# A hybrid decoder layer in fp32 on one core: loads of the last output projection in another ring, the first up weights split ahead, one down product moved to the change of token halves

## The chip, the cores and the metric

The kernel runs on one NeuronCore of a Trainium2 chip. The core has a matmul engine (TensorE, written PE; its weight loads are PEld), a vector engine (VectorE, DVE), an engine for functions and copies (ScalarE, ACT), a general one (GpSimd, POOL) and a queue engine (SyncE, SP) that issues most of the transfers between memory (DRAM) and the on-chip buffer (SBUF). PSUM, eight banks of 128x512 fp32, takes the sums of the matmuls. The engines run beside each other; each works through its own list of instructions in order and waits on semaphores where it needs another's result.

The metric is the time of one execution on the device in microseconds (us). The profile is that of one execution; times in it count from the start of its span.

## The reference

One layer over 2048 tokens of width 1024, all in fp32:

```
h = rmsnorm(x, norm1_w);  p = h @ w_in                  # 1024 -> 3840 columns
o = concat(hgrn2(p[:, :2048]), rwkv7(p[:, 2048:]))      # two recurrent mixers, 512 columns each
x = x + o @ w_out                                       # 1024 x 1024
u = rmsnorm(x, norm2_w) @ w_up                          # 1024 -> 2 x 2816
u = causal_conv(u, conv_w, width 3) + conv_b
x = x + (silu(gate(u)) * val(u)) @ w_down               # 2816 -> 1024
return rmsnorm(x, final_norm_w)
```

The change touches `o @ w_out` for the last 512 tokens, the start of `@ w_up`, and one part of `@ w_down`.

## The kernel before

**Numbers in two parts.** A matmul operand in fp32 is split into a high part (a cast to fp32r on ACT, line 243 or 236) and a low part (the difference, on DVE, line 244 or 237). `mm3` (lines 257 to 261) makes one 128x128 by 128x512 product out of three matmuls: high x high (L259) and the two products of a high and a low part (L260, L261).

**Token blocks and halves.** The 2048 tokens are four blocks of 512 (`b` 0 to 3); blocks 0 and 1 are token half 0, blocks 2 and 3 half 1.

**Phase 1** (`phase1`) makes the mixers for all blocks and the output projections of blocks 0 to 2. Its last output projection, of block 2, runs with matmuls named `pj` beside the end of the mixers of block 3. The mixers' results go to DRAM as `oT[3]`; the last two such stores, of tiles `osq` and `yo`, are issued by POOL. All its SBUF tiles are given back at its end, and the tiles of the second part lie over the same bytes. A new tile waits until every tile of phase 1 that it overlaps has been read for the last time, the whole tile and not only the bytes shared.

**The last output projection** (lines 1142 to 1208, matmuls `wacc`) is that of block 3. For two column halves `dh` and eight k tiles in the order 0, 1, 4, 5, 2, 3, 6, 7 it loads a tile of `w_out` (ring "w") and, in the first half, a tile of `oT[3]` (ring "o"). `rings` puts them in the four slots each of `Bl[2]` and `Bh[2]`, 8 KB tiles whose bytes lie over `hh` and `hl`, the operands that the last `pj` matmuls read. `take` and `weights` split them: `oT` into `Bh[3]`, `Bl[3]`, `Bh[5]`, `Bl[5]`, the weights into `woh`, `wol` (three buffers each, pool `op`). The function `load` chains these loads in the order of the text. Three small loads of `conv_w` and `conv_b` (`crow`) stand ahead of all of them in the program; two transposes of `crow` (`cps`, line 1207) stand behind the last `wacc` matmul.

**The up projection** (`run`, lines 1296 to 1391) works on one token half at a time as a 2x2 block product with seven block products instead of eight (Strassen-Winograd). For each of 22 column tiles `fb` of each half (`n` = 0 to 43) four raw tiles of `w_up` (`uraw`, six buffers, pool `wr2`) give seven operands a11, a12, s2, s1, s3, a22, s4, each split into `uwh`, `uwl` (five buffers) and multiplied with one of the seven prepared activations `Bh[i]`, `Bl[i]`: 12 matmuls a product, 84 an iteration. The accumulators are `ua`, `ub`, `ud`. The last two products and the convolution and gate of iteration n are `late`, called after the first product of iteration n + 1. The gate is a chain on ACT and DVE (lines 1374 to 1388) that ends in stores of `gd`, the input of the down projection.

`build(h, i, kk)` loads a quarter of activation i of half h into the ring `br` (six buffers) and splits it to `Bh[i]`, `Bl[i]`. For half 0 part of this is done in the last output projection and the rest in `run`'s beginning and first iteration. For half 1 the 28 quarters are rebuilt in iterations 21 and 22: a `B[i]` may be overwritten when its last product of half 0 is done; `rebuild(2)` stands before and behind each product. Other small jobs (`aside`: sums for the down projection) are kept out of iterations 20 to 22.

**The down projection** (lines 1396 to 1479) has two token halves `g`, each with seven products `p` of 11 k steps (`KH`), listed in `steps`; a step is two loads of 256 KB, two splits and 12 matmuls, in accumulators `da` or `db` (four banks each, products a, b, a, b, a, a, b). `evict` adds a finished product to rows of x (`xt`). `sums_at` names the 11 steps (13, 18, ... 63) at which the sums for half 1 are made: four loads, four DVE operations, four stores each.

**The order on each engine** is made at build time by a scheduler that goes by the order of the text and by its own estimate of when things are ready; it also gives out PSUM banks. So an instruction can stand earlier on its engine than in the text, if its tiles are free.

Of the kernel before, what the change touches and what calls it, by code (L numbers as in the profile page):

```python
# [18 lines left out]
P = 128  # L19
# [42 lines left out]
def tile_layer(ctx, tc, consts, x, norm1_w, w_in, hg_lb_logits, hg_norm_w, rw_shift_mu, rw_w0, rw_w2,  # L62
# [141 lines left out]
    steps = [(g, p, kk) for g in range(2) for p in range(7) for kk in range(KH)]  # L204
# [901 lines left out]
    with ExitStack() as c2:  # L1106
        wr = c2.enter_context(tc.tile_pool(name="wr2", bufs=1, reuse_waits="tile"))
        hp = c2.enter_context(tc.tile_pool(name="hp2", bufs=1, reuse_waits="tile"))
        hr = c2.enter_context(tc.tile_pool(name="hr2", bufs=1, reuse_waits="tile"))
        B_ = {}  # L1110
        for nm in ("h0", "h1", "h3", "l3", "h2", "l2", "h6", "l0", "l1", "h4", "l4", "l6", "h5", "l5"):
            B_[nm] = hp.tile([P, 4, BLK], F32 if nm[1] == "2" else F32R, tag="B" + nm, name="B" + nm)
# [29 lines left out]
        with tc.tile_pool(name="op", bufs=1, reuse_waits="tile") as op_:  # L1142
            crow = [op_.tile([88, P], F32, name=f"crow{i}") for i in range(2)]
            dma(crow[0], conv_w[0, 0:2, :].rearrange("w (k p) -> (w k) p", p=P))
            dma(crow[1][0:44, :], conv_w[0, 2:3, :].rearrange("w (k p) -> (w k) p", p=P))
            dma(crow[1][44:88, :], conv_b.rearrange("w (k p) -> (w k) p", p=P))
            b = NBLK - 1
            ohl = {}
# [12 lines left out]
            def ring(nm, src):  # L1161

                t_, n_ = rings[nm]
                v = t_[:, len(n_) % 4, :]
# [17 lines left out]
            for dh in range(2):  # L1182
                accs = [pst("wacc") for _ in range(4)]
                for n, k in enumerate((0, 1, 4, 5, 2, 3, 6, 7)):
# [3 lines left out]
                    if n == 5:  # L1188
                        for i in range(4):
                            t0 = b * BLK + i * P  # L1190
                            xt[i] = op_.tile([P, 512], F32, tag="xh", name="xh", bufs=6)
                            load(xt[i], x[0, t0:t0 + P, dh * 512:dh * 512 + 512])
                    if dh == 1 and n == 4:
                        A0 = up_raw(0)
# [10 lines left out]
            for i, (lo_, hi_) in enumerate(((0, 88), (88, 176))):  # L1205
                vps = pst("cps")
                TE.transpose(vps[:, 0:88], crow[i], ident[0:88, 0:88])
                V.tensor_copy(cvt[:, lo_:hi_], vps[:, 0:88])


        with tc.tile_pool(name="up", bufs=1, reuse_waits="tile") as up:
# [74 lines left out]
            def down_start():  # L1286
# [3 lines left out]
                for s_ in range(3):  # L1290
                    lhs, rhs = (split(up, t_, [P, BLK], "uw", 5) for t_ in raws[s_])
# [3 lines left out]

            def run():
                for kk in range(4):
                    build(0, 3, kk)
                loader[0] = dma
# [8 lines left out]
                for n in range(2 * NFF + 1):  # L1308
                    h, fb = n // NFF, n % NFF
                    if n < 2 * NFF:  # L1310
# [3 lines left out]
                        def operand(nm, src, ops=ops):  # L1314
                            ops[nm] = split(up, src, [P, 4, P], "uw", 5)
                            rebuild(2)

                        def prod(acc, nm, bi, first, n=n, ops=ops):
# [10 lines left out]
                            aside(n)  # L1329

# [5 lines left out]
                        acc_a, acc_b, acc_d = pst("ua"), pst("ub"), pst("ud")  # L1336
                        operand("a11", a11)
                        prod(acc_a, "a11", 0, True)
# [6 lines left out]
                    cv = up.tile([P, 16 + 2 * BLK], F32, tag="cv", name="cv", bufs=2)[:, 0:2 + 2 * BLK]  # L1345
# [50 lines left out]
    with tc.tile_pool(name="dn", bufs=1, reuse_waits="tile") as dn:  # L1396
# [59 lines left out]
        for s_ in range(3, N):  # L1456
# [17 lines left out]
            if pend and kk != KH - 1:  # L1474
                pend.pop(0)()
# [35 lines left out]
```

## Time and profile before

| | |
|---|---|
| time, median of 3 runs | 2752.34 us (2749.94 to 2759.56) |
| profiled execution, its own time | 2757.5 us |
| span of its profile | 2755.7 us |
| PE busy | 2647.8 us (96%) |
| DVE busy | 1898.6 us (69%) |
| ACT busy | 1350.4 us (49%) |
| first and last `wacc` matmul | 1397.80 and 1443.82 us |
| first `ua` matmul | 1447.89 us |
| change of token halves (iterations 21 and 22) | 1864.99 to 1919.49 us |
| first `db` matmul (second product of the down projection) | about 2347.5 us |

A row of the timeline reads: start in us, duration in us, engine, line, operation, tile written <- tiles read, shape, number of instructions merged; in brackets the idle time of the engine before it and what ended that. Matmuls overlap, so the time that one takes from the stream is the distance of two starts, not its duration. A row of the windows reads: stretch, length, then for each engine its busy time and number of instructions, the granted clock of PE as a share of full speed, the busy share of the DMA engines and GB/s.

### The profile page before, as it was taken

The page shows a single profiled execution, that of the slowest core. Times are in us where ns is not written, and L with a number is a line of the kernel's source. Part 1 is how long each engine was busy: PE and PEld are TensorE (multiplying, and loading weights), DVE is VectorE, ACT ScalarE, POOL GpSimd, SP SyncE. Part 2 cuts the span into 40 slices and gives each one's busy share as a digit, 9 for nine tenths or more (in the row PEclk, how much of TensorE's full clock was granted, in tenths as well). Part 3 has the DMA queues.
Part 4 walks back from the last instruction along what each step waited for, and adds up shares of the span by engine and source line. Part 5 has one row for each costly group of instructions (what it writes and reads, how often), then busy time and mean ns, then how long its engine had stood idle before and what let it go on. Part 6 is the DMA issues. An engine that isn't in the chain of part 4 may idle for free.

```text
span 2755.7 us, 47958 instructions
## 1 busy us (share of the span) xinstructions
PE 2647.8 (96%) x18059; PEld 2107.5 (76%) x18059; DVE 1898.6 (69%) x3665; ACT 1350.4 (49%) x2164; POOL 368.3 (13%) x660
## 2 busy tenths in 40 slices
PE   7999999989999999999989999998999999999998
PEld 6777777767777767778667788886888888877887
DVE  4856556565456664657657889988997786667656
ACT  5546443444544444344446755455455555445444
POOL 6433222212321113222100000000000000000000
PEclk9999999999999999999999999999999999999999
DMA  8645544355663546844575367746662224999865
GB/s 301 202 152 166 165 138 131 115 146 173 217 176 104 152 146 203 286 138 123 161 273 160 114 205 258 242 148 218 223 228 77 88 85 144 327 327 313 285 196 184
DMA packets 364285, 515.78 MB, mean 187 GB/s; under 512 B 97311, under 2 KB 193941, under 8 KB 364053
## 3 DMA queue, kind: packets, MB, share of 16 engines
q1 hardware_dynamic: 312113, 343.29, 38.6%
q0 software_dynamic: 51872, 169.41, 18.9%
q8 instruction: 142, 2.33, 0.3%
q14 instruction: 90, 0.74, 0.1%
q10 hardware_dynamic: 68, 0.02, 0.0%
HBM read 375.22 MB, written 137.36 MB: 186 GB/s over the span
## 4 chain that ended last, share of the span: by engine, by line
PE 73%; DMA 8%; DVE 7%; issue 5%; ACT 4%; SPq 1%; POOL 1%; DVEq 0%; ACTq 0%; POOLq 0%
PE pj L259 8%; PE pj L260 7%; PE pj L261 7%; PE ua L261 5%; PE ua L259 5%; PE ua L260 5%; PE ud L259 3%; PE ud L260 3%; PE ud L261 3%; PE da L260 2%; PE da L261 2%; PE da L259 2%; PE hg L970 2%; PE db L259 2%; PE db L261 2%
## 5 line engine op out<-in xcount | busy, mean ns | idle before, releaser
L259 PE MATMUL pj<-hh,wh 128*128 128x512 f32 x960 | 404.9, 422 | 0.7 <-ACT hh L117 0.7
L261 PE MATMUL pj<-hh,wl 128*128 128x512 f32 x960 | 380.6, 397 | 0.0
L260 PE MATMUL pj<-hl,wh 128*128 128x512 f32 x960 | 380.6, 397 | 0.0
L259 PE MATMUL ua<-Bh,uwh 128*128 128x512 f32 x704 | 278.6, 396 | 13.8 <-ACT uwh L243 13.1
L261 PE MATMUL ua<-Bh,uwl 128*128 128x512 f32 x704 | 276.9, 394 | 0.9 <-DVE uwl L244 0.9
L260 PE MATMUL ua<-Bl,uwh 128*128 128x512 f32 x704 | 276.4, 393 | 0.0
L259 PEld LDWEIGHTS pj<-hh,wh 128*128 128x128 f32 x960 | 182.4, 190 | 54.2 <-issue 11.8
L260 PEld LDWEIGHTS pj<-hl,wh 128*128 128x128 f32 x960 | 182.6, 190 | 39.7 <-issue 6.2
L261 PEld LDWEIGHTS pj<-hh,wl 128*128 128x128 f32 x960 | 182.2, 190 | 40.1 <-issue 0.4
L243 ACT CAST uwh<-uraw 128x512 fp32r<-128x512 f32 x220 | 134.8, 618 | 145.9 <-PE ua L260 73.2
L243 ACT CAST dah<-draw 128x512 fp32r<-128x512 f32 x151 | 93.8, 621 | 184.1 <-PE da L260 50.5
L244 DVE TENSOR_TENSOR uwl<-uraw,uwh 128x512 fp32r<-128x512 f32 x220 | 146.7, 684 | 47.5 <-ACT uwh L243 47.3
L244 DVE TENSOR_TENSOR dal<-draw,dah 128x512 fp32r<-128x512 f32 x151 | 104.0, 689 | 107.3 <-ACT dah L243 107.2
L259 PEld LDWEIGHTS ua<-Bh,uwh 128*128 128x128 f32 x704 | 133.6, 190 | 43.1 <-ACT uwh L243 13.7
L261 PEld LDWEIGHTS ua<-Bh,uwl 128*128 128x128 f32 x704 | 133.5, 190 | 30.6 <-DVE uwl L244 2.7
L260 PEld LDWEIGHTS ua<-Bl,uwh 128*128 128x128 f32 x704 | 133.6, 190 | 27.3
L259 PE MATMUL ud<-Bh,uwh 128*128 128x512 f32 x352 | 137.9, 392 | 1.9 <-DVE cv L1362 1.9
L261 PE MATMUL ud<-Bh,uwl 128*128 128x512 f32 x352 | 137.1, 389 | 0.0
L260 PE MATMUL ud<-Bl,uwh 128*128 128x512 f32 x352 | 137.0, 389 | 0.0
L260 PE MATMUL da<-dbl,dah 128*128 128x512 f32 x340 | 133.8, 394 | 0.6 <-DVE dbl L244 0.5
L261 PE MATMUL da<-dbh,dal 128*128 128x512 f32 x340 | 133.3, 392 | 0.0
L259 PE MATMUL da<-dbh,dah 128*128 128x512 f32 x340 | 128.3, 391 | 2.4 <-ACT dbh L243 2.3
(558 smaller groups left out, 6036.7 us busy)
## 6 DMA issues: line engine op xcount, KB each, us to landing
uraw<-in_w_up_dram SPq DMA_DIRECT2D x176, 256.0 KB, 3.3
woraw<-in_w_out_dram POOLq DMA_DIRECT2D x96, 256.0 KB, 3.6
draw<-Sg SPq DMA_DIRECT2D x88, 256.0 KB, 3.1
draw<-Tw SPq DMA_DIRECT2D x88, 256.0 KB, 3.0
gd<-y SPq DMA_DIRECT2D x86, 256.0 KB, 2.9
xt<-x1d SPq DMA_DIRECT2D x32, 512.0 KB, 6.0
draw<-gd SPq DMA_DIRECT2D x63, 256.0 KB, 4.8
draw<-in_w_down_dram SPq DMA_DIRECT2D x63, 256.0 KB, 5.3
```

The costliest lines, as they stand in the source:

```text
L243: S.copy(hi, src)
L244: V.tensor_sub(lo, src, hi.bitcast(F32))
L259: TE.matmul(acc, lh, rh, start=first, stop=False, skip_group_check=skip)
L260: TE.matmul(acc, lh, rl, start=False, stop=False, skip_group_check=skip)
L261: TE.matmul(acc, ll, rh, start=False, stop=last, skip_group_check=skip)
L970: TE.matmul(o, kt[:, t0:t0 + 64], qs, start=True, stop=True, tile_position=(0, e * 64))
```

## The change

Three places change.

1. *Last output projection.* The first three loads of each ring go to `uraw` buffers of pool `wr2` in place of `Bl[2]` and `Bh[2]`. That pool's six buffers lie over the tile `xt`/`ohl` of phase 1. The tiles `h4`, `l4` and `h3`, `l3` change places in the list of activations, so that `Bh[3]`, `Bl[3]` no longer lie over `hh` but over `wl`'s fourth buffer and stage tiles. The three `crow` loads move behind six k tiles of the first column half, and the two transposes of `crow` into the second half. Two PSUM tiles that nothing uses are asked for first (`skip`).
2. *First up weights.* The pool of `uwh`, `uwl` (20 KB in each partition) is opened ahead of the output projection's pool `op`, which moves up by these bytes. In iteration 0 the split of a11 stands ahead of the last four builds.
3. *One down product.* Product (0, 1), the 11 steps of token half 0 that multiply rows 1408 to 2815 of the gate's output of block 0 with the matching part of `w_down`, leaves `steps`. The generator `between` makes it in iterations 21 and 22 of the up projection, one step behind each of 11 products, with the splits in the `uw` ring and the raw tiles in `br`; its four sums are copied by ACT to `br` tiles and stored in DRAM (`M2`). In the down projection they are loaded again in the first step of product (0, 2) and added to `xt` in steps 5 to 8. `acc_b` and `acc_d` are asked for after `late` in place of before.

```
--- before.py
+++ after.py
@@ -201,7 +201,8 @@
           ("b", 3, (1, 1)))
-    steps = [(g, p, kk) for g in range(2) for p in range(7) for kk in range(KH)]
+    steps = [(g, p, kk) for g in range(2) for p in range(7) for kk in range(KH) if (g, p) != (0, 1)]
+    M2 = [dp.tile([P, BLK], F32, name=f"M2{i}") for i in range(4)]
@@ -1107,8 +1108,9 @@
         hr = c2.enter_context(tc.tile_pool(name="hr2", bufs=1, reuse_waits="tile"))
+        uw = c2.enter_context(tc.tile_pool(name="uw2", bufs=1, reuse_waits="tile"))
         B_ = {}
-        for nm in ("h0", "h1", "h3", "l3", "h2", "l2", "h6", "l0", "l1", "h4", "l4", "l6", "h5", "l5"):
+        for nm in ("h0", "h1", "h4", "l4", "h2", "l2", "h6", "l0", "l1", "h3", "l3", "l6", "h5", "l5"):
             B_[nm] = hp.tile([P, 4, BLK], F32 if nm[1] == "2" else F32R, tag="B" + nm, name="B" + nm)
@@ -1141,10 +1143,14 @@
             crow = [op_.tile([88, P], F32, name=f"crow{i}") for i in range(2)]
-            dma(crow[0], conv_w[0, 0:2, :].rearrange("w (k p) -> (w k) p", p=P))
-            dma(crow[1][0:44, :], conv_w[0, 2:3, :].rearrange("w (k p) -> (w k) p", p=P))
-            dma(crow[1][44:88, :], conv_b.rearrange("w (k p) -> (w k) p", p=P))
+            def rows_of_conv():
+                load(crow[0], conv_w[0, 0:2, :].rearrange("w (k p) -> (w k) p", p=P))
+                load(crow[1][0:44, :], conv_w[0, 2:3, :].rearrange("w (k p) -> (w k) p", p=P))
+                load(crow[1][44:88, :], conv_b.rearrange("w (k p) -> (w k) p", p=P))
+
             b = NBLK - 1
+            for _ in range(2):
+                pst("skip")
             ohl = {}
@@ -1161,7 +1167,10 @@
                 t_, n_ = rings[nm]
-                v = t_[:, len(n_) % 4, :]
+                if len(n_) < 3:
+                    v = wr.tile([P, 4, P], F32, tag="uraw", name="uraw", bufs=6).rearrange("p k c -> p (k c)")
+                else:
+                    v = t_[:, len(n_) % 4, :]
                 n_.append(0)
@@ -1190,7 +1199,13 @@
                             load(xt[i], x[0, t0:t0 + P, dh * 512:dh * 512 + 512])
+                    if dh == 0 and n == 6:
+                        rows_of_conv()
                     if dh == 1 and n == 4:
+                        for i, (lo_, hi_) in enumerate(((0, 88), (88, 176))):
+                            vps = pst("cps")
+                            TE.transpose(vps[:, 0:88], crow[i], ident[0:88, 0:88])
+                            V.tensor_copy(cvt[:, lo_:hi_], vps[:, 0:88])
                         A0 = up_raw(0)
@@ -1202,10 +1217,6 @@
                     dma(x1d[b][i * P:(i + 1) * P, dh * 512:dh * 512 + 512], xt[i])
-            for i, (lo_, hi_) in enumerate(((0, 88), (88, 176))):
-                vps = pst("cps")
-                TE.transpose(vps[:, 0:88], crow[i], ident[0:88, 0:88])
-                V.tensor_copy(cvt[:, lo_:hi_], vps[:, 0:88])
@@ -1288,15 +1299,30 @@
                 for s_ in range(3):
-                    lhs, rhs = (split(up, t_, [P, BLK], "uw", 5) for t_ in raws[s_])
+                    lhs, rhs = (split(uw, t_, [P, BLK], "uw", 5) for t_ in raws[s_])
                     for i in range(4):
+            def between():
+
+                accs = [pst("fa") for _ in range(4)]
+                for kk in range(KH):
+                    lhs, rhs = (split(uw, raw_(v), [P, BLK], "uw", 5)
+                                for v in (krows(gd_[0], 1, kk), wd_quarter(1, 0, kk)))
+                    for i in range(4):
+                        mm3(accs[i], [t_[:, i * P:(i + 1) * P] for t_ in lhs], rhs, kk == 0, kk == KH - 1, True)
+                    if kk == KH - 1:
+                        break
+                    yield
+                for i in range(4):
+                    t_ = raw_(None)
+                    act(t_, accs[i], AF.Copy)
+                    dma(M2[i], t_)
+                yield
+
             def run():
-                for kk in range(4):
-                    build(0, 3, kk)
-                loader[0] = dma
+                fill_ = between()
                 late, lag = None, []
@@ -1312,7 +1338,7 @@
                         def operand(nm, src, ops=ops):
-                            ops[nm] = split(up, src, [P, 4, P], "uw", 5)
+                            ops[nm] = split(uw, src, [P, 4, P], "uw", 5)
                             rebuild(2)
@@ -1327,14 +1353,20 @@
                             aside(n)
+                            if n == NFF - 1 and bi != 0 or n == NFF and bi in (0, 1, 4, 3, 5):
+                                next(fill_)
-                        acc_a, acc_b, acc_d = pst("ua"), pst("ub"), pst("ud")
+                        acc_a = pst("ua")
                         operand("a11", a11)
+                        if n == 0:
+                            for kk in range(4):
+                                build(0, 3, kk)
+                            loader[0] = dma
                         prod(acc_a, "a11", 0, True)
@@ -1343,6 +1375,7 @@
                     cv = up.tile([P, 16 + 2 * BLK], F32, tag="cv", name="cv", bufs=2)[:, 0:2 + 2 * BLK]
+                    acc_b, acc_d = pst("ub"), pst("ud")
                     operand("a12", a12)
@@ -1394,7 +1427,7 @@
     with tc.tile_pool(name="dn", bufs=1, reuse_waits="tile") as dn:
-        ops, xts, pend, fin = {}, {}, [], []
+        ops, xts, pend, m2 = {}, {}, [], {}
         N = len(steps)
@@ -1410,7 +1443,7 @@
                 raws[s_] = d_loads(s_, d_raw("draw"))
-                if p == 0 and kk in (4, 6, 8, 10) or p == 1 and kk in (1, 3, 5, 7):
+                if p == 0 and kk in (4, 6, 8, 10) or p == 2 - g and kk in (1, 3, 5, 7):
                     u, i = (0, kk // 2 - 2) if p == 0 else (1, kk // 2)
@@ -1455,7 +1488,7 @@
             g, p, kk = steps[s_]
-            if "b" not in accs and p == 1:
+            if "b" not in accs and p == 3:
                 accs["b"] = [pst("db") for _ in range(4)]
@@ -1473,6 +1506,13 @@
                 pend.pop(0)()
+            if (g, p) == (0, 2):
+                if kk == 0:
+                    for i in range(4):
+                        m2[i] = dn.tile([P, BLK], F32, tag="m2", name="m2", bufs=4)
+                        dma(m2[i], M2[i])
+                if 5 <= kk < 9:
+                    add(0, 0, 0, kk - 5, m2[kk - 5])
             if s_ in sums_at:
```

## The prediction

> **What bounds the kernel now.** I read the page first: the share of each engine and the chain that ended last.
>
> ```profile
> PE 2647.8 (96%) x18059; PEld 2107.5 (76%) x18059; DVE 1898.6 (69%) x3665; ACT 1350.4 (49%) x2164; POOL 368.3 (13%) x660
> ...
> PE 73%; DMA 8%; DVE 7%; issue 5%; ACT 4%; SPq 1%; POOL 1%; DVEq 0%; ACTq 0%; POOLq 0%
> ```
>
> PE carries the kernel. No matmul is taken away here, so only time in which PE waits, or runs at a lower clock, can be won. Next I read the waits of PE from 1300 us to the end.
>
> ```profile
> PE ua L259 <- ACT uwh L243: 13.1, 2, 9.6
> PE wacc L259 <- ACT Bh L236: 7.3, 1, 7.3
> PE da L259 <- ACT dbh L243: 2.3, 2, 1.2
> ```
>
> The large ones are three places: before the first `wacc`, before the first `ua`, and at the change of token halves. The timeline of PE gives each its price. First the steady step: two starts of `wacc`, 36 matmuls apart.
>
> ```profile
> 1435.66 0.39 PE L261 MATMUL wacc<-woh,Bl 128*128 128x512 f32 x1
> ...
> 1443.82 0.39 PE L261 MATMUL wacc<-woh,Bl 128*128 128x512 f32 x1
> ```
>
> 8.16/36 is 0.2267 us a matmul, 2.72 a product of 12. *Place 1*, the start of the last output projection:
>
> ```profile
> 1390.16 0.39 PE L261 MATMUL pj<-wh,hl 128*128 128x512 f32 x1
> 1397.80 0.79 PE L259 MATMUL wacc<-woh,Bh 128*128 128x512 f32 x1 [7.25 <-ACT Bh L236]
> ...
> 1402.66 0.63 PE L261 MATMUL wacc<-woh,Bl 128*128 128x512 f32 x1
> 1403.09 0.50 PE L259 MATMUL wacc<-woh,Bh 128*128 128x512 f32 x1
> ```
>
> From 1390.16 to 1403.09 lie 13 steps, 2.95 us at full pace; it took 12.93. The loss is 10.0 us: the wait, and some 2.4 us because the matmuls up to 1402.66 come 0.43 us apart, at half the clock. *Place 2*, the start of the up projection, from 1443.82:
>
> ```profile
> 1447.89 0.79 PE L259 MATMUL ua<-Bh,uwh 128*128 128x512 f32 x1 [3.53 <-ACT uwh L243]
> ...
> 1450.01 0.80 PE L261 MATMUL ua<-Bh,uwl 128*128 128x512 f32 x1 [0.90 <-DVE uwl L244]
> ...
> 1454.71 0.40 PE L260 MATMUL ub<-Bl,uwh 128*128 128x512 f32 x1
> ```
>
> 10.89 us for 14 steps and two transposes (about 3.5): a loss of 7.4. *Place 3*, the change of halves, between the first `ub` matmuls of iterations 20, 21 and 23:
>
> ```profile
> 1845.95 0.39 PE L259 MATMUL ub<-Bh,uwh 128*128 128x512 f32 x1
> ...
> 1864.99 0.39 PE L259 MATMUL ub<-Bh,uwh 128*128 128x512 f32 x1
> ...
> 1919.49 0.39 PE L259 MATMUL ub<-Bh,uwh 128*128 128x512 f32 x1
> ```
>
> An undisturbed iteration takes 19.04 us; the next two took 54.50 in place of 38.08: a loss of 16.4. The three places hold 33.8 us.
>
> **The change part by part. Place 1.** What PE waited for is a chain that starts only when the last `pj` matmul is done, because the first raw tiles lie over its operands:
>
> ```profile
> SPq L401 <- DVE xh L399: 12.7, 2, 12.4
> ...
> 1391.81 0.65 SPq L1144 DMA_DIRECT2D crow<-in_conv_w_dram  x1
> ...
> 1393.62 0.36 SPq L1153 DMA_DIRECT2D Bl<-in_w_out_dram  x1
> 1394.03 0.43 SPq L1153 DMA_DIRECT2D Bh<-oT  x1
> ...
> 1397.13 0.62 ACT L236 CAST Bh<-Bh 128x512 fp32r<-128x512 f32 x1 [0.25 <-DMA Bh<-oT]
> ```
>
> In the new kernel the six raw tiles can be there long before: `ohl`, over which they lie, is read for the last time half a `pj` projection earlier, and SP stood still for 12.4 us ahead of 1390.6 (the first row). The three `crow` loads (1.8 us of SP, 1391.81 to 1393.62) leave the head of the queue too; later they stand among loads with several steps of lead, and I cost them at nothing. Two waits stay. `Bh[3]` now lies over the fourth `wl` buffer, whose last reader is the last `pj` product: cast at about 1390.6, first matmul at 1391.2, 0.8 us lost. And `op` moved up by 20 KB, so that `wol` lies over `yo`, which a late store reads:
>
> ```profile
> 1389.68 0.72 POOL L919 DMA_DIRECT2D oT<-yo  x1 [2.63 <-DVE yo L918]
> ...
> DMA to landing us min/median/max: 2.9/3.2/5.6
> ...
> 1396.91 0.69 DVE L237 TENSOR_TENSOR wol<-Bl,woh 128x512 fp32r<-128x512 f32 x1 [5.64 <-ACT woh L236]
> ```
>
> It lands at about 1392.9, `wol` follows at 1393.6, and the second matmul waits 2.2 us; `Bl`'s low part behind it on DVE costs 0.4. That is 3.4 us of waiting. Does the clock fall for so short a wait? At the change of halves it did:
>
> ```profile
> 1879.80 0.50 PE L259 MATMUL ud<-Bh,uwh 128*128 128x512 f32 x1 [1.94 <-DVE cv L1362]
> ...
> 1881.62 0.63 PE L259 MATMUL ua<-Bh,uwh 128*128 128x512 f32 x1
> ...
> 1883.33 0.63 PE L260 MATMUL ua<-Bl,uwh 128*128 128x512 f32 x1
> ```
>
> A wait of 1.94 us was followed by eight steps of 0.43, about 1.6 us. I take it: 5.0 left of 10.0, a gain of 5.0. Ends: 1.0 left (no wait for `yo`), 10.0 left (the stage is near its transfers' limit, below).
>
> The Trainium skill, "TensorE: Matmul & The Clock Gate", section "HAM oscillation — how this bites in real kernels", gives as a rule that only idle gaps above about 3.4 us throttle the array; the 1.94 us row speaks against it. By that rule the short waits left in the three places would keep the full clock, 3 x 1.6 us less than I forecast.
>
> **Place 2.** The split of a11 had to wait for the bytes of `op` and stood behind four builds; now it has bytes of its own and can be done while `wacc` runs. `ua` can follow the last `wacc` at once. Next comes DVE, which was full there:
>
> ```profile
> 1436.00:1456.00 20.00, 15.57 (x58) 12.03 (x57) 18.97 (x34) 14.77 (x26) 0.00 (x0) 0.83 0.95 317
> ...
> 1455.87 0.68 DVE L244 TENSOR_TENSOR uwl<-s,uwh 128x512 fp32r<-128x512 f32 x1
> ```
>
> The low part of s2 was ready at 1456.6. PE without its wait wants it two products behind 1444.1, at 1449.6. The moved split and the moved `cvt` copies free 1 us of DVE, its own gaps another 1; if the order stays, s2 is some 5 us late. If the scheduler puts it ahead of builds not needed yet, it is not late at all. Ends of what is left: 0 and 7.4; I take the middle, 3.5 with its half clock. Gain 3.9.
>
> **Place 3.** Here PE ended up waiting for DVE:
>
> ```profile
> 1864.99:1919.49 54.50, 42.76 (x170) 33.53 (x168) 48.14 (x76) 32.19 (x53) 0.00 (x0) 0.87 0.67 219
> ...
> 1906.00:1926.00 20.00, 20.00 (x90) 16.56 (x89) 15.77 (x24) 9.66 (x15) 0.00 (x0) 1.00 0.76 261
> ...
> L237 DVE TENSOR_TENSOR Bl<-br,Bh x28: 679/684/693, 1858.9 to 1898.4; 128x512 fp32r<-128x512 f32 x28
> L1382 DVE SCALAR_TENSOR_TENSOR y<-cv,cvt,y 128x1024 f32<-128x1024 f32 x42 | 53.9, 1282 | 29.8 <-ACT y L117 29.8
> ...
> 1900.28 1.14 ACT L243 CAST uwh<-s 128x512 fp32r<-128x512 f32 x2 [3.69 <-DVE s L1352]
> ```
>
> DVE's ordinary share is 15.77 in 20 us, 15.0 in an iteration. Two iterations and 28 low parts (0.60 from start to start) need 30.0 + 16.8 = 46.8 us, PE's matmuls only 38.1: 8.7 of the 16.4 us lost are want of DVE, the rest order and clock. The change brings 132 matmuls, 29.9 us, and 22 splits: 22 x 0.60 = 13.2 us of DVE, about as much of ACT, which had 22 us free. PE then has 68.0 us of work, DVE 60.0: the want is gone. In the down projection the same 29.9 us of PE and 22 splits fall away, so the moved product costs nothing by itself. What is left is order. Between s4 of iteration 21 and s2 of 22, DVE has the gate (L1374 to L1388: an addition and five passes of some 1.2 us from start to start, 6.6 us), two sums and splits (3.0) while PE has one product and one step, 5.4. The two passes on `cv` can run earlier (2.4), so 1.8 us may be late; as much again for a wait like that of L1362, and one fall of the clock: 5.0 left of 16.4, gain 11.4. Ends: 0 left, or all 16.4 and more (the slower rival).
>
> The step's loads: 22 of 256 KB, 5.8 MB in 70 us, 83 GB/s more where 219 were moved; the `br` ring of six took about one load a us (the nine loads of the row below), 50 loads fit in the 60 us from the first step to the last. The last step reads gate row 21, which is stored only behind the gate; SP holds what is queued behind that load, the next `uraw`.
>
> ```profile
> 1875.93 7.18 SPq L1120 DMA_DIRECT2D br<-Ts  x9
> ...
> 1889.24 0.69 DVE L1374 TENSOR_TENSOR cg<-ud,m 128x512 f32<-128x512 f32 x1
> ...
> 1897.88 0.80 SPq L1390 DMA_DIRECT2D gd<-y  x2
> ```
>
> The store came 8.6 us behind L1374; with landing, load and split some 16, and PE comes there seven products behind s4, 19 us. No cost; if DVE is 3 us later, that is PE's wait. The four ACT copies and four stores of `M2` lie beside iteration 23.
>
> **Down projection.** Four loads of `M2` and four additions from SBUF replace four from PSUM: nothing. Products 0 and 2 now follow each other in the same `da` banks: nine matmuls, 2.0 us, cover an addition of 0.69. The sums of half 1 keep their step numbers and run beside products 2 to 6. DMA is 93% busy there:
>
> ```profile
> 2347.00:2441.00 94.00, 93.42 (x405) 75.20 (x405) 63.09 (x99) 39.56 (x64) 0.00 (x0) 1.00 0.93 325
> ```
>
> The few waits for `dbh` (2.3 us, above) stay; 0, with 3 either way.
>
> **Sum.** 5.0 + 3.9 + 11.4 = 20.3 us less. The profiled execution took 2757.5 us (its span 2755.7 and 1.8 around it), which gives 2737.2; the median shown, 2752.34, is 5.2 below it: 2732.
>
> **The rivals.** *Short waits at full clock* (the rule above): 2727; its price is 3 x 1.6 us off the forecast, and only a short wait without a slow stretch behind it would speak for it, 0.08. *Nearly all closed*, 3 us left of 33.8: 2721; for it, that the scheduler may move s2 and the gate; against it, DVE near full in both places, 0.15. *The start does not gain*: the output projection is bound by its transfers, so that PE only waits later. For it:
>
> ```profile
> 1390.55:1444.05 53.50, 46.25 (x193) 37.93 (x193) 29.93 (x48) 24.89 (x42) 0.00 (x0) 0.90 0.91 310
> ```
>
> 16.6 MB move in that stage; 1.6 MB go ahead of it, and 15.0 MB at 310 to 340 GB/s are 44 to 48 us beside 43.5 of matmuls. Then only place 3 pays: 2741, 0.13. *Place 3 does not gain*: 2743, 0.08. *The change does nothing* (the scheduler moves no load ahead and waits move elsewhere): 2752, 0.07. *Slower: the down steps are not covered.* The five `uw` buffers now serve three splits for each product and step, so a split may start only when PE has left the buffer five back, 5.4 us ahead of its use, in place of 10.9. Cast and low part take 1.3; if DVE's order puts the gate's 6.6 us between, PE waits up to 2.5 us. That hits two of 11 steps by my count; with w us at each of 11 steps, the gain is gone at w = 2.3 (25 us) and the kernel slower by over 0.3% from w = 3.1. At 3.0 to 3.5 it ends at 2760 to 2766. 0.10.
>
> **How the numbers follow.** The forecast, 2732, has 0.39; its own range is 2723 to 2741. A measurement of this kernel can tell about 0.3% from no change, 8.3 us: 2744 to 2761 is the same. Faster: 0.39 + 0.08 + 0.15 + 0.13 and half of the 0.08 (2743 is at the edge), 0.79. Same: that half and 0.07, 0.11. Slower 0.10. The range 2715 to 2749 leaves out the slower case, most of no change, and a little below.
>
> **What would show it.** Place 1: loads of `oT` and `w_out` on SP well ahead of 1390, a first `wacc` within 1.5 us of the last `pj`, a second that waits for `wol`. Place 2: `ua` right behind the last `wacc`, a wait ahead of s2. Place 3: first `ub` of iteration 21 to that of 23 in 68 to 75 us, DVE below 92%. Down projection: 29.9 us shorter. I would be wrong if waits of over 1 us stand at most of the 11 steps, if `wacc` waits for transfers in its middle, or if the waits for `dbh` grow.

## The result, and the profile after

The changed kernel takes 2753.83 us (median of 14 runs, 2742.40 to 2763.72), the kernel before 2754.06 us in 14 runs beside it: a ratio of 1.0000, with an interval of 0.9987 to 1.0013. No difference can be measured. The forecast was 2732, its range 2715 to 2749.

The profiled execution took 2742.4 us and is the fastest of the 14. Its last `pj` matmul starts 10.1 us sooner than in the profile of before, in code that the change doesn't touch. Over all 14 profiles of this study that point lies anywhere between 1379.9 and 1396.0 us (mean 1387.6 in the ten kernels with the early loads, 1383.9 in the four without), so I take the 10.1 us for scatter; that the early loads cost a few us ahead of that point is not excluded. I compare stages from that matmul on, by the start times of the last matmul of each kind (us); the last column goes to the end of the last VectorE instruction:

| kernel | last `pj` to last `wacc` | to first `ua` | up projection, to last `ud` | down projection, to last `db` | last `pj` to end |
|---|---|---|---|---|---|
| before | 53.66 | 4.08 | 870.24 | 429.71 | 1361.87 |
| after | 51.01 | 0.23 | 891.39 | 410.11 | 1356.91 |

The up projection has taken in 29.9 us of matmuls and grown by 21.2; the down projection has lost 29.9 us of matmuls and shrunk by 19.6. From the last `pj` to the end 5.0 us are won instead of 20.3.

The page's first part and the chain that ended last, and the waits of PE from 1300 us to the end, of the kernel after (columns as for before):

```profile
PE 2638.4 (96%) x18059; PEld 2098.8 (77%) x18059; DVE 1899.1 (69%) x3665; ACT 1349.5 (49%) x2168; POOL 368.9 (13%) x660
...
PE 68%; DMA 10%; DVE 8%; issue 6%; ACT 5%; SPq 1%; POOL 1%; DVEq 0%; ACTq 0%; POOLq 0%
```

```profile
PE da L260 <- ACT dbh L244: 6.5, 5, 1.8
PE db L260 <- ACT dbh L244: 4.5, 4, 2.6
PE wacc L260 <- ACT Bh L237: 4.1, 1, 4.1
PE ua L260 <- ACT uwh L244: 3.1, 1, 3.1
PE fa L261 <- DVE uwl L245: 2.7, 2, 1.6
```

The wait of 9.6 us at the change of halves is gone, the one before `wacc` has fallen from 7.3 to 4.1. At the head of the list now stand the waits for `dbh` in the down projection: 11.0 us, where they were 3.8 before (2.3 of `da`, 1.5 of `db`). The DMA's share of the chain is 10% for 8%.

*Place 1*, timeline of after, first SP and ACT, then PE:

```profile
1328.94 0.33 SPq L1159 DMA_DIRECT2D uraw<-in_w_out_dram  x1
...
1335.18 0.43 SPq L1159 DMA_DIRECT2D uraw<-oT  x1
...
1382.84 1.14 ACT L237 CAST woh<-uraw 128x512 fp32r<-128x512 f32 x2 [4.93 <-DMA oT<-yo]
1383.88 1.66 ACT L237 CAST Bh<-uraw 128x512 fp32r<-128x512 f32 x3
...
1380.02 0.39 PE L262 MATMUL pj<-wh,hl 128*128 128x512 f32 x1
1384.55 0.80 PE L260 MATMUL wacc<-woh,Bh 128*128 128x512 f32 x1 [4.15 <-ACT Bh L237]
...
1390.90 0.40 PE L260 MATMUL wacc<-woh,Bh 128*128 128x512 f32 x1
```

The six raw loads were issued 45 us ahead. But ACT casts three `woh` before the first `Bh`, and behind the first of them (at 1377.29) it stands 4.93 us for the store of `yo`, with the other two and the `Bh` casts behind it. Then the matmuls run at half clock until about 1390.5. From 1380.02 to 1390.90 lie 16 steps, 3.63 us at full pace, in 10.88: 7.25 us lost, for 10.0 before.

*Place 2*, timeline of PE:

```profile
1431.03 0.39 PE L262 MATMUL wacc<-woh,Bl 128*128 128x512 f32 x1
1431.25 0.39 PE L260 MATMUL ua<-Bh,uwh 128*128 128x512 f32 x1
...
1439.92 0.50 PE L260 MATMUL ua<-Bh,uwh 128*128 128x512 f32 x1 [3.06 <-ACT uwh L244]
...
1445.34 0.39 PE L261 MATMUL ua<-Bl,uwh 128*128 128x512 f32 x1
```

`ua` follows the last `wacc` at once, and PE waits for the split of s2 instead. 37 steps, 8.39 us, in 14.31: 5.9 lost, for 7.4.

*Place 3*, first `ub` of iterations 21 and 23, and the stretch between them in the windows:

```profile
1851.82 0.39 PE L260 MATMUL ub<-Bh,uwh 128*128 128x512 f32 x1
...
1924.29 0.39 PE L260 MATMUL ub<-Bh,uwh 128*128 128x512 f32 x1
```

```profile
1851.82:1924.29 72.47, 68.96 (x302) 56.00 (x300) 58.91 (x91) 47.33 (x79) 0.00 (x0) 1.00 0.66 218
```

72.47 us with 68.0 us of matmuls: 4.5 lost, for 16.4. DVE is busy 81%.

*Down projection.* Rows of the tile view give the first and last start of a group; first before, then after:

```profile
L261 PE MATMUL ud<-Bh,uwl x352: 389/389/397, 1460.4 to 2318.1; 128*128 128x512 f32 x176
L261 PE MATMUL db<-dbh,dal x264: 387/389/402, 2347.9 to 2747.8; 128*128 128x512 f32 x132
```

```profile
L262 PE MATMUL ud<-Bh,uwl x352: 388/389/424, 1445.8 to 2322.6; 128*128 128x512 f32 x176
L262 PE MATMUL db<-dbh,dal x220: 387/389/628, 2387.3 to 2732.7; 128*128 128x512 f32 x110
```

The windows of before and after, 200 us each from 30 us behind the last `ud` on:

```profile
2348.00:2548.00 200.00, 195.12 (x833) 155.70 (x832) 140.65 (x214) 94.75 (x168) 0.00 (x0) 0.99 0.93 322
```

```profile
2352.00:2552.00 200.00, 188.38 (x800) 149.10 (x799) 140.24 (x213) 92.09 (x165) 0.00 (x0) 0.99 0.95 337
```

PE, busy 195.12 of 200 us before, is busy 188.38 after, while the DMA engines went from 93 to 95% and from 322 to 337 GB/s. That share alone does not separate them. Here are 50 us of the kernel before, in which PE lost nothing, and the 50 us of the changed kernel in which it lost most, 5.85 us:

```profile
2325.00:2375.00 50.00, 49.96 (x221) 40.98 (x220) 32.16 (x49) 24.46 (x38) 1.10 (x2) 1.00 0.95 334
```

```profile
2475.00:2525.00 50.00, 44.15 (x179) 33.84 (x179) 35.75 (x54) 26.82 (x56) 0.00 (x0) 0.97 0.92 325
```

SP's queue shows another thing that the operand loads wait for. The stores of the sums (L199) stand in it until VectorE has made the sums, and the loads behind them stand too: 50.1 us in the changed kernel, 51.0 in the kernel before. The largest of the four such rows of each, from 2310 to 2560 us, first before, then after:

```profile
SPq L199 <- DVE sraw L194: 34.0, 11, 3.7
```

```profile
SPq L199 <- DVE sraw L194: 32.9, 11, 3.5
```

### The profile page after: what moved, and what is told of

Read it like the earlier page. It is cut to its first block, busy times and chain, and to the rows that moved or that the text cites. A ratio compares the mean times of both kernels' runs of the same rounds, so it can differ in the third digit from the quotient of the medians.

```text
span 2740.6 us, 47945 instructions
## 1 busy us (share of the span) xinstructions
PE 2638.4 (96%) x18059; PEld 2098.8 (77%) x18059; DVE 1899.1 (69%) x3665; ACT 1349.5 (49%) x2168; POOL 368.9 (13%) x660
## 4 chain that ended last, share of the span: by engine, by line
PE 68%; DMA 10%; DVE 8%; issue 6%; ACT 5%; SPq 1%; POOL 1%; DVEq 0%; ACTq 0%; POOLq 0%
PE pj L260 8%; PE pj L261 7%; PE pj L262 7%; PE ua L262 5%; PE ua L260 5%; PE ua L261 5%; PE ud L262 2%; PE ud L260 2%; PE ud L261 2%; PE da L261 2%; PE da L260 2%; PE da L262 2%; PE hg L971 2%; DMA woraw<-in_w_out_dram 2%; PE ub L262 1%
## 5 line engine op out<-in xcount | busy, mean ns | idle before, releaser
L260 PEld LDWEIGHTS pj<-hh,wh 128*128 128x128 f32 x960 | 181.7, 189 | 54.7 <-issue 11.8
L244 ACT CAST dah<-draw 128x512 fp32r<-128x512 f32 x140 | 87.0, 622 | 184.7 <-DMA draw<-Sg 60.0
L245 DVE TENSOR_TENSOR dal<-draw,dah 128x512 fp32r<-128x512 f32 x140 | 96.6, 690 | 103.8 <-ACT dah L244 103.5
```

Of the source, the lines that this page charges most:

```text
L244: S.copy(hi, src)
L245: V.tensor_sub(lo, src, hi.bitcast(F32))
L260: TE.matmul(acc, lh, rh, start=first, stop=False, skip_group_check=skip)
```

## The experiments

**The changed kernel once more, and each half of the change alone.** `e1_again` is the changed kernel. `e2_product_only` keeps the moved product and undoes the edits at the start of both stages; `e3_start_only` does the reverse.

```diff
 e2_product_only, against the changed kernel:
-                if len(n_) < 3:
-                    v = wr.tile([P, 4, P], F32, tag="uraw", name="uraw", bufs=6).rearrange("p k c -> p (k c)")
-                else:
-                    v = t_[:, len(n_) % 4, :]
+                v = t_[:, len(n_) % 4, :]
...
-                            ops[nm] = split(uw, src, [P, 4, P], "uw", 5)
+                            ops[nm] = split(up, src, [P, 4, P], "uw", 5)
 e3_start_only, against the changed kernel:
-    steps = [(g, p, kk) for g in range(2) for p in range(7) for kk in range(KH) if (g, p) != (0, 1)]
+    steps = [(g, p, kk) for g in range(2) for p in range(7) for kk in range(KH)]
...
-                            if n == NFF - 1 and bi != 0 or n == NFF and bi in (0, 1, 4, 3, 5):
-                                next(fill_)
```

> The changed kernel once more, to see which stretches repeat. In its first profile the part from the last pj matmul to the end of the last matmul took 1356.9 us, in the kernel before 1361.9; phase 1 ended 10.1 us earlier, at 1379.8 in place of 1389.9. Theory T (the gain of some 16 us at the start and at the change of halves is given back in the down projection, 10 us, and phase 1 differs by chance): second part 1357 +- 3, phase 1 anywhere from 1378 to 1395, time within 0.3% of before. Rival P (the early loads make phase 1 itself shorter or longer): phase 1 ends near 1380 again.

> The kernel before with the third part of the change alone: the down product in iterations 21 and 22. T: the two iterations take 72 us in place of 68 + 16.4, a gain of 12, and the down projection is 20 us shorter in place of 29.9, so that about 2 us are won, 2752. Rival D (the down projection loses for another reason than its transfers, or nothing): 2742, 12 us won.

> The kernel before with the first two parts of the change and without the third. T: only the two starts gain, 2.7 + 1.4 us, 2750; the down projection as before. Rival P (the early loads disturb phase 1): slower than before, 2757 or more.

| kernel | last `pj` to last `wacc` | to first `ua` | up | down | last `pj` to end | ratio to before |
|---|---|---|---|---|---|---|
| e1_again | 50.70 | 0.23 | 892.69 | 411.61 | 1359.41 | 1.0014 [0.9997, 1.0031] |
| e2_product_only | 53.85 | 5.18 | 889.03 | 413.31 | 1365.55 | 1.0009 [0.9994, 1.0025] |
| e3_start_only | 50.83 | 0.23 | 874.11 | 429.90 | 1359.24 | 0.9993 [0.9976, 1.0010] |

The picture repeats, and the last `pj` of `e1_again` starts at 1391.55 us, so the early one of the first profile does not. Both kernels with the moved product have a down projection of 410 to 413 us where 399.8 was forecast, whatever their start. The start alone wins 6.7 us up to the first `ua` and gives 3.9 of it back in the up projection, so it is worth 2.6. The moved product alone is not worth anything: its gain at the change of halves (it needs 74.6 us there, a gain of 9.8) goes in the down projection, which is 13.5 us longer than 399.8.

**The sums of half 1 further apart.** My first theory was that the moved product makes the sums (`g_sums`, L194 to L197) too dense against the steps. One sum in seven steps instead of five:

```diff
-        sums_at = {KH + 5 * j + 2: j for j in range(KH)}
+        sums_at = {KH + 7 * j + 2: j for j in range(KH)}
```

> The changed kernel with the sums of half 1 seven steps apart in the down projection in place of five (steps 13 to 83). T: 2 MB of sums in 19 us in place of 13.6 us brings the transfers from about 350 GB/s wanted to about 305, below the 330 seen; of some 20 us of waits in the down projection 10 go, 2744. Rival D: the waits stay, 2754.

Slower than the kernel before, 1.0027 [1.0008, 1.0045]; the down projection took 416.85 us. Waits of PE in it:

```profile
PE da L260 <- ACT dbh L244: 10.2, 6, 4.2
PE da L260 <- DVE xt L1459: 4.3, 1, 4.3
```

The wait of 4.3 us ends at 2473.8 us, in the stretch where the sums were thinned: DVE's addition L1459 stood behind a sum whose loads were late, and PE behind it. Of the 18 us of PE's waits 9.3 lie from 2555 us on, where the last sums now meet the residual tiles (512 KB each) that half 1 loads at its start. Density by steps was not the cause, or not by itself; the theory fell in that form. What stayed open: is it the bytes of the sums, or the order of so many instructions in SP's and DVE's queues?

**A quarter of the bytes, as many instructions.** Half 1's operands are read from half 0's sums in this run, so half 1's result is left out; it ran once.

```diff
-        a11, a12, a21, a22 = (tile_(krows(gd_[2 * g + u], q, kk)) for u in range(2) for q in range(2))
+        a11, a12, a21, a22 = (tile_(krows(gd_[2 * g + u], q, kk)[:, 0:128]) for u in range(2) for q in range(2))
...
-            dma(krows(Sg[g][i], 0, kk), t_)
+            dma(krows(Sg[g][i], 0, kk)[:, 0:128], t_)
```

> The changed kernel, with the sums of token half 1 during the down projection (g_sums) at a quarter of their width: the same instructions in the same order on every queue, but each load, store and VectorE step moves 128 of 512 columns, so 23.1 MB of transfers (11 x 8 of 256 KB) become 5.8 MB. Half 1's operands are read from half 0's sums; half 1's result is left out in that. From the last matmul of the up projection to the last of the down projection the changed kernel took 410.1 to 411.6 us, of which 143 steps of 2.72 us are 389.0 and waits the rest. Theory (the transfers of the stretch are its bound, not the number or order of instructions): the waits of TensorE over 0.5 us, 15.6 us together, fall under 4, and the stretch takes 396 to 402 us; the DMA share between 2400 and 2550 us falls under 0.85. Rival (SyncE's queue in order, with sum stores that wait for VectorE ahead of operand loads): the same instructions still stand ahead, waits of 10 us or more stay, 407 to 412 us.

Waits of PE in the down projection, and the same 200 us in the windows:

```profile
PE da L260 <- ACT dbh L244: 1.7, 2, 1.5
PE da L261 <- DVE dbl L245: 0.5, 2, 0.2
```

```profile
2352.00:2552.00 200.00, 200.00 (x884) 165.62 (x883) 139.10 (x236) 101.99 (x183) 0.00 (x0) 1.00 0.85 285
```

The down projection took 391.23 us, better than the 396 to 402 expected, and PE is busy 200 us of 200. The DMA share fell to 0.85, where less than that was expected. As many instructions of the sums stand in the queues as before, so their number is not what cost the time; their size is. What the size acts through this run doesn't tell. VectorE was busy for 70% of the stretch in either kernel, but its steps of a sum are shorter (0.29 us for 0.69), SP stands 28.3 us at the stores of the sums instead of 50.1, and the order is not quite the same, since the scheduler sets some of the sums' stores and VectorE steps at other places. So the expected order of the queues did not hold, and neither full DMA engines nor SP's queue is ruled out. One wait of 1.5 us stays, 7 us behind the last `ud` and well ahead of the first sum.

**Both kernels without the sums.** The price of the product that was moved, when its stretch has room (half 1 reads half 0's sums again, so its result is left out):

```diff
-        sums_at = {KH + 5 * j + 2: j for j in range(KH)}
+        sums_at = {}
...
-        return (tile_(krows(Sg[g][a], 0, kk) if isinstance(a, int) else krows(gd_[2 * g + a[0]], a[1], kk)),
+        return (tile_(krows(Sg[0][a], 0, kk) if isinstance(a, int) else krows(gd_[2 * g + a[0]], a[1], kk)),
```

> The changed kernel without the sums of token half 1 (half 1 reads the sums of half 0; so half 1's result is left out). Theory (transfers): the down stretch takes 394 to 400 us instead of 410 to 412, and the run some 10 to 16 us less than the changed kernel. Rival (the change of products from a to a and the tile release bring the waits, the sums do not): over 406 us.

> The kernel before without the sums of token half 1 (left out as in the run beside it). Theory: its down stretch loses less, since it was 429.7 with 154 steps (418.9) and 4.5 us of waits over 0.5 us: 424 to 429 us, so that the product that is moved away is worth its whole 29.9 us there (28 to 31 between the two kernels without sums, where 18 to 20 were measured with them). Rival: the difference stays at 18 to 20 us.

Tile view and windows, first the changed kernel, then the kernel before, without the sums:

```profile
L262 PE MATMUL ud<-Bh,uwl x352: 387/389/398, 1450.3 to 2327.8; 128*128 128x512 f32 x176
L262 PE MATMUL db<-dbh,dal x220: 388/389/389, 2387.6 to 2716.0; 128*128 128x512 f32 x110
```

```profile
2358.00:2558.00 200.00, 200.00 (x884) 165.59 (x883) 125.42 (x190) 98.17 (x183) 0.00 (x0) 1.00 0.77 255
```

```profile
L261 PE MATMUL ud<-Bh,uwl x352: 388/389/398, 1450.5 to 2309.1; 128*128 128x512 f32 x176
L261 PE MATMUL db<-dbh,dal x264: 388/389/389, 2338.9 to 2727.2; 128*128 128x512 f32 x132
```

```profile
2339.00:2539.00 200.00, 200.00 (x884) 165.60 (x883) 122.13 (x185) 96.97 (x182) 0.00 (x0) 1.00 0.75 246
```

388.2 us for 143 steps and 418.1 us for 154: 2.715 us a step in both, no wait, and a difference of 29.9 us. Both are shorter than expected (394 and 424 at the least), the difference is the one that the theory gave. So it is the sums that take the gain, though leaving them out frees the transfers, VectorE and SP's queue all at once. The moved product is worth its whole price once they are gone; with them the down projection loses 11.6 us in the kernel before (429.7 less 418.1) and 21.9 in the changed one (410.1 less 388.2; 23.4 in `e1_again`). The runs took 0.9913 [0.9893, 0.9933] and 0.9953 [0.9934, 0.9973] of before.

**The start of the last output projection.** The six tiles of x go ahead of the split weights, which so no longer lie over `yo`:

```diff
-        with tc.tile_pool(name="op", bufs=1, reuse_waits="tile") as op_:
+        with tc.tile_pool(name="ox", bufs=1, reuse_waits="tile") as ox, tc.tile_pool(name="op", bufs=1, reuse_waits="tile") as op_:
+            for i in range(6):
+                ox.tile([P, 512], F32, tag="xh", name="xh", bufs=6)
+            pad = ox.tile([P, 512], F32, name="pad")
...
-                            xt[i] = op_.tile([P, 512], F32, tag="xh", name="xh", bufs=6)
+                            xt[i] = ox.tile([P, 512], F32, tag="xh", name="xh", bufs=6)
```

> The changed kernel with the six x tiles of the last output projection put ahead of its split weights, so that no split weight lies over the tile whose store ends phase 1. Theory for the start of the last output projection (ScalarE splits the third weight, which waits for that store, ahead of the Bh on which the first product waits): the first wacc stands about 1 us behind the last pj instead of 4.53, the loss up to the first full rate falls from 7.3 to 2 to 4 us, and pj to the end takes 3 to 5 us less than the 1356.9 and 1359.4 us of the changed kernel: 0.9982 to 0.9988 of it, some 0.9985 of before. Rival (the weights' loads or the Bh buffers are late in any case): first wacc at 4 us or later, no gain in pj to the end.

```profile
1385.87 0.39 PE L262 MATMUL pj<-wh,hl 128*128 128x512 f32 x1
1386.71 0.49 PE L260 MATMUL wacc<-woh,Bh 128*128 128x512 f32 x1 [0.46 <-ACT Bh L237]
1387.63 0.50 PE L261 MATMUL wacc<-wol,Bh 128*128 128x512 f32 x1 [0.43 <-DVE wol L238]
1389.44 0.80 PE L262 MATMUL wacc<-woh,Bl 128*128 128x512 f32 x1 [1.30 <-DVE Bl L238]
1390.03 0.63 PE L260 MATMUL wacc<-woh,Bh 128*128 128x512 f32 x1
...
1395.86 0.39 PE L262 MATMUL wacc<-woh,Bl 128*128 128x512 f32 x1
```

The reason given is right, the first `wacc` follows in 0.84 us. The gain is smaller than expected: DVE has three `wol` and three `Bl` to make and PE waits for the first of each, and the clock is halved until about 1395.6 as it was after one long wait. 18 steps, 4.08 us, took 9.99: 5.9 lost for 7.25, and last `pj` to last `wacc` 49.69 us for 51.01. From the last `pj` to the end it took 1358.0 us, between the two profiles of the changed kernel; 0.9986 [0.9969, 1.0003] of before.

**The sums where the transfers are light.** The page of after shows little traffic late in the up projection; its slices are 68.5 us long, and the last nine iterations lie in the 32nd to 34th, at 90, 86 and 76 GB/s:

```profile
GB/s 303 199 166 166 165 136 130 117 148 183 214 167 111 148 152 204 311 123 119 182 265 139 140 199 258 240 148 207 264 232 113 90 86 76 323 333 327 298 194 184
```

Eight of the 11 sums as side jobs there, like those of half 0:

```diff
+    EARLY = 8
...
+            for kk in range(EARLY):
+                four([krows(gd_[2 + u], q, kk) for u, q in QB], s_make, s_out(lambda i, kk=kk: krows(Sg[1][i], 0, kk)))
...
-        sums_at = {KH + 5 * j + 2: j for j in range(KH)}
+        sums_at = {KH + 5 * j + 2: j for j in range(EARLY, KH)}
```

> The changed kernel with 8 of the 11 sums of token half 1 made in the last nine iterations of the up projection, where 76 to 90 GB/s move, as side jobs like those of half 0; three stay in the down projection. All of the computation is done. Theory (the down stretch is bound by its transfers while the sums run): the stretch takes 389 to 394 us instead of 410 to 412 (388.2 with no sums), the up projection 891 to 895 us (891.4 and 892.7), and pj to the end 1335 to 1342 us instead of 1357 to 1359; the run about 0.993 of before (0.991 to 0.995). Rival (the sums cost VectorE and the ring of raw tiles in the up projection what they cost the down projection): up 900 us or more, pj to the end 1350 us or more, within 0.3% of before.

> The same move of 8 sums in the kernel before. Theory: its down stretch falls from 429.7 to 418 to 422 us (418.1 with no sums), pj to the end from 1361.9 to 1350 to 1355 us, 0.995 to 0.997 of before; the kernel of the change with the same move is then 13 to 17 us shorter from pj to the end, what the prediction gave the change (20.3 us) less what the start still loses. Rival (the gain is the change's own and not the sums'): the kernel before stays at 1360 to 1363 us.

> The 8 sums in the up projection and the six x tiles ahead of the split weights, in one kernel. Theory: the gains add, 1.3 us at the start of the last output projection (the first run with those tiles: last wacc at 49.69 us for 51.01) and some 20 us in the down stretch: pj to the end 1334 to 1341 us, 0.991 to 0.994 of before. Rival: 1.3 us of the start is taken back at the first s2 (its wait grew from 3.1 to 3.8 us) and the kernel stands with the one beside it within 0.1%.

| kernel | up | down | last `pj` to end | median | ratio to before |
|---|---|---|---|---|---|
| e9, the changed kernel | 903.57 | 392.27 | 1349.86 | 2740.88 | 0.9939 [0.9918, 0.9961] |
| e10, the kernel before | 880.21 | 418.11 | 1361.87 | 2751.72 | 0.9981 [0.9963, 1.0000] |
| e11, e9 with e8's tiles | 903.30 | 392.26 | 1348.39 | 2739.47 | 0.9938 [0.9917, 0.9959] |

The down projection does what was expected in all three. But the up projection takes 10 to 12 us of it back, as the rival for e9 had it (900 us or more); in the kernel before that leaves nothing, from the last `pj` to the end. With eight of the sums out of the way the change is worth 12.0 us there (13 to 17 expected), and e9 (four runs) and e11 (six) are faster than the kernel before by 0.6%. The changed kernel can't be told from the kernel before, so they are faster than it too, though the two were not run side by side. The tiles seem to add 1.5 us from the last `pj` to the end; the medians of e9 and e11 can't be told apart. PE's waits from 2000 to 2340 us in e9 are 8.3 of the 12 us, and VectorE waits beside them from 2100 us on:

```profile
PE ua L261 <- ACT m L117: 8.3, 7, 1.7
```

```profile
DVE br L1269 <- DMA br<-gd: 24.7, 8, 4.7
```

The changed kernel has neither wait there. VectorE waits at every sum for its loads. The last try gave the loads more time, one iteration and three more places:

```diff
+                side[-3:-3] = [None, None]
```

> The kernel with 8 early sums and the x tiles ahead, each sum one iteration later and with three free places for one between its loads and its first VectorE step. With the sums right behind the gate's stores the up projection took 903.3 us for 890.6: VectorE waited 24.7 us for the sums' loads (8 waits, up to 4.7 us), whose issue on SyncE waited for the store of the gate's rows, and TensorE waited 8.3 us for ScalarE's copies behind it. Theory (the loads come late, the VectorE work itself fits): these VectorE waits fall under 5 us, the up projection takes 891 to 895 us, the down stretch stays at 392 to 394 us, pj to the end 1336 to 1341 us, 0.989 to 0.992 of before. Rival (four more VectorE steps an iteration are too many): up 899 us or more, pj to the end 1345 us or more.

It did not help: up 900.82 us, down 394.43, 1348.01 from the last `pj` to the end, 0.9954 [0.9938, 0.9970].

```profile
DVE br L1272 <- DMA br<-gd: 27.0, 8, 3.6
...
SPq L1140 <- DVE uwl L246: 88.9, 23, 7.9
```

The same waits remain. The second row is SP's queue: the loads of the next up weights stand for their buffers, and the sums' loads behind them in the same queue. That this holds the sums up is read from the rows and not tested; how the sums could be made there for nothing stays open.

## Why the prediction was wrong

Term by term, in us of gain, from the first profile after (in brackets `e1_again`, where it was read):

| term | forecast | measured |
|---|---|---|
| place 1 | 5.0 | 2.75 |
| place 2 | 3.9 | 1.5 |
| place 3 | 11.4 | 11.9 (9.9) |
| down projection, beside the 29.9 | 0 ("with 3 either way") | -10.3 (-11.8) |
| sum | 20.3 | 5.9; 5.0 (2.5) from the last `pj` to the end |

**The down projection is the step that failed.** The prediction had it 29.9 us shorter and said: "The few waits for `dbh` (2.3 us, above) stay; 0, with 3 either way." It priced the product there by PE's time, put the sums of half 1 at nothing because they "keep their step numbers", and quoted in the sentence before that DMA is 93% busy at 325 GB/s. But the kernel before already lost 11.6 us to the sums in that stretch, of which the row of 2.3 us shows a fifth, and the changed kernel loses 21.9. Without the sums the product is worth its 29.9 us; with them 16.4 to 19.6 were measured. The prediction's own sign came: the waits for `dbh` grew, from 3.8 to 11.0 us.

How the sums take the time is argued here and not shown. One reading is their bytes. By them the moved product is an estimated 14 to 15 us: 22 loads of 256 KB less 4 of `M2`, 4.7 MB, at 322 to 337 GB/s. Per step of 2.715 us two loads of 256 KB ask for 193 GB/s, and a sum in every five steps for 154 more: 347 in all, ahead of `M2` and the residual tiles, and less than that was moved on average in both kernels. The Trainium skill, "Perfetto Trace Analysis", section "Roofline", puts the practical ceiling of a single core at some 435 GB/s; by that the 347 would have fitted and the moved product would have been worth its 29.9 us. In this trace the DMA engines were 93 to 95% busy at a mean of 322 to 337 GB/s, with single slices of 5 us at up to 406; no run here shows where the ceiling of this mix lies. Against the bytes alone stand the two rows of 50 us above: PE lost nothing at 95% and 334 GB/s, and 5.85 us at 92% and 325. The other reading is the order: operand loads that stand in SP's queue behind the stores of a sum. At one sum of the changed kernel the next operand loads were issued at 2492.5 us, 8.9 us behind the ones before them with the four stores of the sum between, and PE waited 0.8 us at 2496.7. A run with the sums at full size and their stores out of SP's queue would tell the two apart.

Why the changed kernel loses ten us more to the sums than the kernel before did can be placed in the trace. Of the 11.6 us that PE loses in the 200 us of the windows, 7.6 lie between 2480 and 2540 us. The sums keep their step numbers, but the half is 11 steps shorter, so half 0's finished rows now leave while sums are still made: the first of eight output stores of 512 KB is issued at 2485.2 us and the last sum is stored at 2526.9. In the kernel before the first output store is issued at 2514.7, right behind the last sum (2514.3). Half 1's residual tiles come later still, from 2527.3 us on; the run with the sums seven apart, which overlap with those tiles, is slower. No run moves the last sums alone, so this cause is read from the rows and not tested.

**Place 1** was right in its parts and wrong in a queue. The loads came early, and the store of `yo` was the wait left over. The prediction let it reach PE through `wol` at the second matmul, 2.2 us. But ACT runs its six casts in order, `woh` three times first, so the store held back `Bh` and the first matmul, 4.15 us. The run with tiles of their own shows it.

**Place 2**: the wait for a11 is gone, the one for s2 came in its place as forecast, at 5.9 lost for 3.5. The 3.06 us are within the "some 5 us late" that the prediction named; it then took 3.5, about the middle of its ends. The run with the start alone shows that 3.9 us more go later in the up projection, for a reason that no run shows.

**Place 3** was right: 72.47 us in the "68 to 75", DVE at 81% for "below 92%", waits of over 1 us at two of the 11 steps as counted (1.13 and 1.57), and one of 0.81 at a third. `e1_again` and `e2_product_only` need 74.5 and 74.6 us, at the end of that range. The slower rival, waits of 2 to 3 us at each step, fell. The rival "the start does not gain" has half of its loss, for another reason than the transfers it named; "the change does nothing" gave the time, though not because loads or waits failed to move.

**The median.** The forecast was taken from the profile of before less 5.2 us. The interval of the ratio reaches down to 0.9987, 3.6 us, so the 5.0 us of the first profile are more than the times bear out and the 2.5 us of `e1_again` can hide in the scatter ahead of the last `pj`. That any of it is won is read from two profiles and not shown by the times.

## What to carry to other kernels

Before work is taken out of a stretch, ask what else runs in it: where PE waits there and the DMA engines are at 93%, PE's time is not the price of the work. Leave the other load out of both kernels once (here the sums), and see whether the price comes back, before it is moved. A wait for a late store reaches whatever its engine has queued behind it, so follow the engine's order and not the matmul that needs the tile. Where runs scatter by more than the change is worth, compare stages from a common mark.

## What the runs showed of the hardware that was not expected

Transfers of 256 KB, loads and stores mixed, kept the DMA engines 93 to 95% busy at 322 to 337 GB/s over 200 us, with PE losing 5 to 12 us; at 246 to 291 GB/s (75 to 86%) PE lost nothing. The share alone does not decide it: 50 us at 95% and 334 GB/s in the kernel before cost PE 0.04 us.

The clock does not follow the longest wait alone. Three waits of 0.46, 0.43 and 1.30 us within 3.6 us (`e8_own_tiles`) were followed by steps of 0.43 us for 5.5 us, much as the one of 4.15 us was; at the change of halves waits of 1.13, 0.81 and 1.57 us, at 1862.6, 1867.8 and 1898.3 us, left the granted clock at 1.00. The Trainium skill, "TensorE: Matmul & The Clock Gate", section "HAM oscillation — how this bites in real kernels", gives idle gaps above some 3.4 us as what throttles the array; the first row speaks against it, the second does not.
